# A hybrid attention and gated-linear-attention block on one Trainium2 core: another way to spread c, another order of first loads, products of zeros on TensorE, and the last output columns in two halves

## The chip, the core and the metric

The kernel runs on one core of one Trainium2 chip (trn2). The metric is the device time of one execution in microseconds (us); of several runs the median is given, beside the lowest and the highest. The profile shows one execution on the same core. Engines are named as the profile names them: PE is TensorE (PEld its weight loads), DVE VectorE, ACT ScalarE, POOL GpSimd, SP the engine that issues nearly all DMAs.

## The reference, cut to what matters

```python
mod = silu(c) @ w_cond + b_cond                 # c: (1, 2048), w_cond: (2048, 6144)
shift, scale, gate = split(mod, 3)
h = rms_norm(x) * (1 + scale) + shift           # x: (1, 512, 2048)
proj = h @ w_in                                 # 7200 columns
a_out = dilated_attention(aq, ak, av) * silu(ag)        # 16 heads of 64
g_out = rms_norm(gla_fwd + gla_bwd) * gain * silu(gg)   # 4 heads, dk 128, dv 256
y = concat(a_out, g_out) @ w_out                # (512, 2048) @ (2048, 2048)
out = rms_norm(x + gate * y) * final_gain
```

All is float32. There are 512 tokens and 2048 model columns.

## The kernel before, in words

Each float32 product is done as three products of rounded parts: a helper `three` (lines 169 to 171) adds high times high, low times high and high times low. The high part is an ACT copy into the rounded type, the low part a DVE subtraction.

**The start.** c is loaded as one row (line 181) and bcond, the bias of the conditioning, right after it (line 190). c must stand on all 128 partitions: for each quarter of 512 columns ACT rounds the row (L236), DVE takes the rest (L237), and two products with a row of ones (L238, L239) spread high and low part; ACT puts their sum through SiLU into `sb` (L240). `bcond[:, 16:32]` gets 1 added on DVE (L191). The columns of w_cond for scale come as 128x2048 tiles `cb`, one for each of 16 k-tiles; DVE multiplies a tile by `sb` and sums along the row (`cond_sum`, L244), which gives one column of scale. For k=0 this is done in four quarters. Two small products `pb` (L253) turn the relative bias into a row, which DVE combines with a constant (`bias_row_out`, L257) and ACT stores to DRAM (`grow`, L259).

**Stage a** multiplies x, scaled by (1+scale) but not yet normalised, with the 1024 value columns of w_in: for each k-tile ACT makes the high part of u (`u_high`, L347), DVE the low part (`u_low`, L350), ACT and DVE the parts of the weight tile (`w_high`, L388; `w_low`, L397; for k=0 in two halves), and PE does 8 groups j of three products (`sta`), all 8 sums staying in PSUM. DVE adds up squares of x on the way (`add_square`, L358). **Stage b** does the same for 8 further groups (`stb`) with the fully normalised h (`h_high` L378, `h_low` L381), after the sums of stage a were copied out (`v_out`, L412) and the inverse norms were made (`rstd`, L370 and L371).

The order in which ACT, DVE, SP and POOL run these steps is written out by a planner, `_plan`: each step is a task with an engine, an assumed duration, the tasks it needs, a priority, and buffers that it takes or gives back; the planner runs a clock over them, from given times at which each engine is ready, and records an order. Each engine then runs in that order, so a step that waits holds up all behind it on its engine. Weight tiles have 3 buffers for their parts and 4 for the raw load; `b8` is a pool of 8 large tiles.

**The middle** (attention, gated linear attention, gates) follows in units of 512 columns (`unit`), which the change leaves as they are.

**The end.** The output product runs in four units of 512 columns, o0 to o3. o3 runs for tokens 0 to 255, then for 128 tokens, then for the last 128. Behind each group of 128 tokens stands `finish`: DVE multiplies by the gate (L1009) and adds x (L1010), ACT squares and sums (L1012), takes Ln and Exp (L1033, L1034) for the inverse norm r, then four parts of 512 columns are multiplied by r: part 3 on DVE (L1036), parts 0 and 1 on ACT (L1037, L1039), part 2 on POOL (L1038); SP stores the four parts (L1041). In the built order POOL's part is stored first.

Of the kernel before, what the change touches and what calls it, by code (L numbers as in the profile page):

```python
# [133 lines left out]
def block_kernel(ctx: ExitStack, tc: tile.TileContext, a: dict):  # L134
# [50 lines left out]
    onesr = cst.tile([P, P], F32R, tag="ones", name="ones")  # L185
    act(onesr, one, AF.Copy)
    ones = onesr.bitcast(F32)
# [3 lines left out]
    nc.vector.tensor_scalar(bcond[:, 16:32], bcond[:, 16:32], 1.0, None, op0=ALU.add)  # L191
# [30 lines left out]
    cond_load(0, 0)  # L222
    rel = const("rel", [32, NH])
# [7 lines left out]
    c_parts = [T2(f"c_{e}", F32R) for e in range(8)]  # L231
    for j in range(4):
        ch, cl = c_parts[2 * j][64:65, :], c_parts[2 * j + 1][64:65, :]
        src = first[64:65, 512 * j:512 * j + 512]
# [5 lines left out]
        act(sb[:, 512 * j:512 * j + 512], pc, AF.Silu)  # L240

# [13 lines left out]
    def bias_row_out(j):  # L255
        t = first[:NH, 1024 + 512 * j:1536 + 512 * j]
        tt(t, pbs[j][:NH], t, op=ALU.add)  # L257
        if j:
            nc.scalar.dma_start(grow, first[:NH, 1024:2048])  # L259
# [74 lines left out]
    def sums(k, e):  # L334
# [3 lines left out]
        if k == e == 0:  # L338
            to = [part[:, z:z + 1] for z in range(3)] + [dst]
            for z in range(4):  # L340
                c = slice(512 * z, 512 * z + 512)
# [42 lines left out]
    def w_high(st, k):  # L384
        hi = wp.tile([P, 1024], F32R, tag="whi", name=f"s{st}{k}h")
        lo = wp.tile([P, 1024], F32R, tag="wlo", name=f"s{st}{k}l")
        for c in halves(st, k):
            act(hi[:, c], start_w[st, k][:, c], AF.Copy)  # L388
        spl[st, k] = hi, lo

    def halves(st, k):
        return (slice(0, 512), slice(512, 1024)) if (st, k) == ("a", 0) else (slice(0, 1024),)

    def w_low(st, k):
        hi, lo = spl[st, k]
        for c in halves(st, k):
            tt(lo[:, c], start_w[st, k][:, c], hi[:, c].bitcast(F32), op=ALU.subtract)  # L397
# [46 lines left out]
    for i, (st, k) in enumerate(sets[1:], 1):  # L444
# [4 lines left out]
        task(("w", st, k), "DMA", 1.55, [("w",) + sets[i - 1]], 1000.5 - 200 * e - 10 * k,  # L449
             lambda st=st, k=k: start_load(st, k), "raw")  # L450
    for k in range(KT):
        task(("sum", k, 0), "DVE", 2.42 if k else 3.4, [("load", k, 0)], 600 - 2 * k,
# [7 lines left out]
    for i, (st, k) in enumerate(sets):  # L460
        task(("wh", st, k), "ACT", 1.0, [("w", st, k)], 640 - i, lambda st=st, k=k: w_high(st, k), "wts")
# [3 lines left out]
    def mm_task(i):  # L465
        st, k, j = chain[i]
        need = [("ul" if st == "a" else "lo", k), ("wl", st, k)]
# [10 lines left out]
    for z in range(2):  # L478
        task(("row", z), "DVE", 0.66, [("ul", 0)], 950, lambda z=z: bias_row_out(z), None, "b8" if z else None)
# [32 lines left out]
    for i in range(2):  # L512
# [3 lines left out]
                 {"PE": 10.5, "ACT": 9.5, "DVE": 6.0, "POOL": 7.0, "DMA": 8.5})  # L516
# [326 lines left out]
    def unit(name, natural, side=(), rhs=None, lr=None, tiles=range(4)):  # L843
# [3 lines left out]
        ps = [PJ(f"ps_{name}_{i}") for i in tiles]  # L847
        pos, tick, ticks = 0, 0, 16 * len(tiles)
        for q in range(KT // 2):
# [12 lines left out]
            for n, i in enumerate(tiles):  # L862
                for kk in range(2):
                    k = 2 * g + kk
                    rh, rl = (h_hi[:, k, :], h_lo[:, k, :]) if rhs is None else rhs[k]
                    if natural:
                        t = slice(i * P, i * P + P)
                        cw = slice(kk * 512, kk * 512 + 512)
                        three(ps[n], rh[:, t], rl[:, t], hi[:, cw], lo[:, cw], q + kk == 0, q + kk == KT // 2)
# [120 lines left out]
    ssq = cst.tile([P, 4, 4], F32, tag="ssq", name="ssq")  # L990
# [14 lines left out]
    def add_up(i, ps, j):  # L1005

        x_ = x2[i][:, j, :]
        t = T2(f"y{i}{j}")
        tt(t, ps, sb[:, 512 * j:512 * j + 512], op=ALU.mult)  # L1009
        tt(x_, t, x_, op=ALU.add)  # L1010
        sq = T2(f"ysq{i}{j}")
        act(sq, x_, AF.Square, accum_out=ssq[:, i, j:j + 1])  # L1012
        if j < 3:
            nc.gpsimd.tensor_tensor(x_, x_, fgain[j], op=ALU.mult)  # L1014

    for j in range(3):
# [4 lines left out]
        for i in range(4):  # L1021
            add_up(i, ps[i], j)
# [6 lines left out]
    def finish(i, ps):  # L1029

        add_up(i, ps, 3)
# [3 lines left out]
        x_ = x2[i]  # L1035
        stt(x_[:, 3, :], x_[:, 3, :], r, fgain[3], op0=ALU.mult, op1=ALU.mult)  # L1036
        act(x_[:, 0, :], x_[:, 0, :], AF.Copy, scale=r)  # L1037
        nc.gpsimd.tensor_scalar(x_[:, 2, :], x_[:, 2, :], r, 1.0, op0=ALU.mult, op1=ALU.mult)  # L1038
        act(x_[:, 1, :], x_[:, 1, :], AF.Copy, scale=r)  # L1039
        for z in (3, 0, 2, 1):  # L1040
            nc.sync.dma_start(a["out"][i * P:i * P + P, 512 * z:512 * z + 512], x_[:, z, :])  # L1041
# [18 lines left out]
def _constants():  # L1060
# [6 lines left out]
    for window, dil in ((128, 1), (512, 4), (2048, 16)):  # L1067
# [3 lines left out]
    j, i = np.arange(P)[:, None], np.arange(P)[None, :]  # L1071
    rst = np.ones((P, 512), f)
    rst[:, ::P] = 0.0
    return {
        "ident": np.eye(P, dtype=f), "oneh": oneh, "lnm": np.tile(row, (NH, 1)),
# [4 lines left out]
def _layout(x, c, w_cond, b_cond, w_in, gla_gate_up_fwd, gla_gate_bias_fwd, gla_gate_up_bwd,  # L1080
# [6 lines left out]
    r["c"] = np.asarray(c)  # L1087
# [43 lines left out]
```

## Time and profile before

| | us |
|---|---|
| median of 3 runs | 975.26 (973.75 to 977.06) |
| the profiled execution, own time | 973.38 |
| its span in the trace | 971.6 |
| TensorE (PE) busy | 943.0 (97% of the span) |
| DVE busy | 616.6 |
| ACT busy | 441.0 |
| granted clock, mean | 0.997 |

A timeline row gives the start in us from the span's start, the duration in us, the engine, the line of the kernel, the operation, output and inputs, shapes and count (a row with x2 or more covers several that follow each other), and in brackets how long the engine had been idle and what released it. The start of an instruction on DVE or ACT can lie about 0.1 us ahead of the end of the one before it, since they overlap a little; where steps follow each other the text counts from start to start. Matmul durations overlap too, so their pitch is also counted from start to start.

### The profile page before, as it was taken

Reading aid. Unit: us, or ns where it says so; the run is one execution under the profiler, and the core shown is the slowest. Engines: PE = TensorE matmul, PEld = TensorE weight load, DVE = VectorE, ACT = ScalarE, POOL = GpSimd, SP = SyncE. Lnnn points to the kernel's source line nnn. Section 1 sums busy time; section 2 is a strip of 40 time slices with the busy share of each in tenths; the row PEclk is TensorE's granted clock in tenths of the full one; section 3 lists DMA queues with packets and bytes.
Section 4 is the critical chain, followed back from the end, with each engine's and each line's share of the span. In section 5 each row is a group of like instructions: output and inputs, shape, how many; then the busy total and the mean of one; then the engine's idle time right before and its main releaser. Section 6 shows DMA issues by size and latency. Waiting matters only on the chain.

```text
span 971.6 us, 11885 instructions
## 1 busy us (share of the span) xinstructions
PE 943.0 (97%) x4464; PEld 775.7 (80%) x4464; DVE 616.6 (63%) x916; ACT 441.0 (45%) x735; POOL 81.6 (8%) x100
## 2 busy tenths in 40 slices
PE   8999999989999999999999999999999999999996
PEld 4888788878778777778777888888888888888884
DVE  7988999566665676775534647585885352546431
ACT  5443533655655645655413544363744151333222
POOL 0000000011111122012000000000010000202120
PEclk9999999999999999999999999999999999999998
DMA  9998687422222253332444334355465455244013
GB/s 333 414 411 347 238 302 258 133 85 96 92 84 82 85 193 105 126 128 84 146 152 166 121 109 152 130 176 171 139 228 176 152 175 193 87 148 156 22 50 124
DMA packets 42619, 159.56 MB, mean 164 GB/s; under 512 B 5217, under 2 KB 5505, under 8 KB 37825
## 3 DMA queue, kind: packets, MB, share of 16 engines
q1 hardware_dynamic: 42386, 158.48, 47.2%
q8 instruction: 35, 0.57, 0.2%
q10 hardware_dynamic: 176, 0.33, 0.1%
q14 instruction: 22, 0.18, 0.1%
HBM read 154.51 MB, written 4.28 MB: 163 GB/s over the span
## 4 chain that ended last, share of the span: by engine, by line
PE 81%; DVE 8%; DMA 3%; ACT 3%; issue 3%; POOL 1%; SPq 0%; ACTq 0%; DVEq 0%; POOLq 0%
PE ps_o L170 6%; PE ps_o L171 6%; PE ps_o L169 6%; PE sta L169 3%; PE sta L170 3%; PE sta L171 3%; PE stb L171 3%; PE stb L169 3%; PE stb L170 3%; PE ps_qk L169 3%; PE ps_gv L170 3%; PE ps_gv L171 3%; PE ps_gv L169 3%; PE ps_qk L171 3%; PE ps_qk L170 3%
## 5 line engine op out<-in xcount | busy, mean ns | idle before, releaser
L585 POOL TENSOR_SCALAR p<-p,st 128x512 f32<-128x512 f32 x64 | 46.1, 721 | 424.3 <-DVE st L584 407.8
L583 ACT ACTIVATE p<-p,st 128x512 f32<-128x512 f32 x64 | 46.2, 722 | 63.4 <-DVE st L580 63.4
L244 DVE CUSTOM_DVE_ANT_0 cb<-cb,sb,c_bcond 128x2048 f32<-128x2048 f32 (+1 forms) x32 | 73.4, 2294 | 0.0
L602 DVE TENSOR_TENSOR pt<-t,pt 128x512 fp32r<-128x512 f32 x64 | 44.1, 689 | 17.8 <-ACT pt L601 17.8
L597 PE MATMUL t<-c_ident,p 128*128 128x128 f32 x256 | 38.9, 275 | 10.6 <-POOL p L585 10.6
L597 PEld LDWEIGHTS t<-c_ident,p 128*128 128x128 f32 x256 | 30.9, 140 | 22.3 <-POOL p L585 15.4
L580 DVE CUSTOM_DVE_ANT_0 p<-s,g 128x512 f32<-128x512 f32 x64 | 43.6, 686 | 7.0 <-PE s L577 6.1
L601 ACT ACTIVATE pt<-t 128x512 fp32r<-128x512 f32 x64 | 37.8, 591 | 21.1 <-PE t L597 20.5
L244 DVE CUSTOM_DVE_ANT_0 rawg<-rawg,sb,gate 128x1024 f32<-128x1024 f32 x16 | 20.7, 1294 | 27.8 <-DMA rawg<-in_wg 27.8
L611 PEld LDWEIGHTS o<-pt,vv 128*128 128x128 f32 x256 | 34.2, 189 | 3.8 <-DVE pt L602 1.7
L244 DVE CUSTOM_DVE_ANT_0 rawg<-rawg,sb,c_bcond 128x1024 f32<-128x1024 f32 x16 | 20.5, 1283 | 25.2 <-DMA rawg<-in_wg 25.2
L611 PE MATMUL o<-pt,vv 128*128 128x256 f32 x256 | 35.9, 283 | 0.0
L1014 POOL TENSOR_TENSOR x<-x,fgain 128x512 f32<-128x512 f32 x12 | 20.0, 1675 | 183.8 <-ACT ysq L1012 183.8
L1012 ACT ACTIVATE ysq<-x 128x512 f32<-128x512 f32 x16 | 10.1, 632 | 47.1 <-DVE x L1010 44.8
L767 POOL TENSOR_SCALAR dc<-st,sc 128x256 f32<-128x256 f32 x16 | 10.5, 656 | 242.5 <-DVE st L764 237.6
L584 DVE RECIPROCAL st<-st 128x1 f32<-128x1 f32 x64 | 10.4, 162 | 31.3 <-ACT p L583 31.2
L1009 DVE TENSOR_TENSOR y<-ps_o,sb 128x512 f32<-128x512 f32 x16 | 10.9, 684 | 25.9 <-PE ps_o L171 25.9
L576 PE MATMUL s<-ks,qs 128*128 128x512 f32 x64 | 25.3, 395 | 0.2 <-DVE qs L540 0.2
L577 PE MATMUL s<-kl,qs 128*128 128x512 f32 x64 | 25.0, 391 | 0.0
L774 ACT ACTIVATE sq<-st,sc 128x256 f32<-128x256 f32 x24 | 12.2, 509 | 26.2 <-DVE st L769 13.8
L618 DVE TENSOR_TENSOR cat<-o,oh 64x256 f32<-64x256 f32 x32 | 13.3, 415 | 11.9 <-ACT oh L614 11.7
L614 ACT ACTIVATE oh<-o 64x256 f32<-64x256 f32 x32 | 12.2, 380 | 17.3 <-PE o L611 16.5
(1279 smaller groups left out, 2944.6 us busy)
## 6 DMA issues: line engine op xcount, KB each, us to landing
cb<-in_wm SPq DMA_DIRECT2D x31, 1024.0 KB, 7.5
rawg<-in_wg SPq DMA_DIRECT2D x32, 512.0 KB, 3.4
raw_o<-in_w_o SPq DMA_DIRECT2D x32, 512.0 KB, 3.4
raw_qk<-in_w_qk SPq DMA_DIRECT2D x24, 512.0 KB, 3.3
rawb<-in_w_sb SPq DMA_DIRECT2D x16, 512.0 KB, 4.3
rawv<-in_wv SPq DMA_DIRECT2D x16, 512.0 KB, 3.4
raw_gv<-in_w_gv SPq DMA_DIRECT2D x16, 512.0 KB, 3.4
raw_ag<-in_w_ag SPq DMA_DIRECT2D x16, 512.0 KB, 3.4
```

The source lines that it names most:

```text
L169: mm(ps, lh, rh, start=first, stop=False)
L170: mm(ps, ll, rh, start=False, stop=False)
L171: mm(ps, lh, rl, start=False, stop=last)
L244: nc.vector.tensor_tensor_reduce(out=w, in0=w, in1=with_, op0=ALU.mult, op1=ALU.add, scale=1.0, scalar=init, accum_out=dst)
L576: mm(ps, qs[:, q], ks, start=True, stop=False)
L580: nc.vector.tensor_tensor_reduce(out=t, in0=ps, in1=gt[h][:, P * i:P * i + 512], op0=ALU.add, op1=ALU.min, scale=1.0, scalar=3e38, accum_o ...
L583: act(t, t, AF.Exp, bias=st[:, 0:1], scale=-1.0, accum_out=st[:, 1:2])
L585: nc.gpsimd.tensor_scalar(t, t, st[:, 2:3], 1.0, op0=ALU.mult, op1=ALU.mult)
L597: nc.tensor.transpose(pk[:, kt * P:kt * P + P], t[:, kt * P:kt * P + P], ident)
L601: act(hi, src, AF.Copy)
L602: tt(lo, src, hi.bitcast(F32), op=ALU.subtract)
L611: mm(po[:, :256], vv[h // 4][:, kt, h % 4, :], t[:, w, kt, :], start=kt == 0 and w == 0, stop=kt == 3 and w == 1)
```

## The change

At the start:

- c is loaded as 4 rows of 512. A constant `sel` (64 rows, 512 columns, 128 KB) is loaded before it. `crow` has 64 rows, zeros but for the four high parts (rows 0 to 3) and the four low parts (rows 32 to 35); one ACT and one DVE instruction make them. One product of `sel` and `crow` for each quarter replaces the two.
- `idle` is a tile of zeros. PE multiplies zeros by zeros (128x128 by 128x256, float32): three such products before c is ready and four behind the products of c.
- bcond is loaded after the four quarters of the first cb tile instead of before them. The addition to it, and the copy of ones, stand later in the program.
- The first sum runs in three pieces (512, 512, 1024) instead of four.
- The halves of the first weight tile are tasks of their own: the second half is rounded after `u_high(0)`. The weight load of a k-tile now has a lower priority than the cb load of the same k-tile. The store of the bias row is a task of its own on ACT, after `u_high(1)`. The times at which the planner takes the engines to be ready are earlier.

At the end: `finish` puts the multiplications of parts 0 and 2 on DVE and that of part 1 on ACT, none on POOL. The last 128 tokens of o3 run as two units of 256 columns; the first half is added up, squared and multiplied by the final gain while the second half's products run, so that behind the last product only 256 columns go through `add_up`, and there are five stores.

The built order of the changed kernel differs from the old one in two more ways, both the planner's doing. In stage a the weight parts of a k-tile are made for that k-tile and not for the one after it. And at the end of stage a, ACT runs: copies out of groups 0, `sb0h`, groups 1 and 2, rstd, group 3, rcol, groups 4, 5, 6, `sb1h`, group 7, then `h_high(0)`. Before, both `sb0h` and `sb1h` stood ahead of group 0, and `h_high(0)` ahead of group 7.

```diff
-    nc.sync.dma_start(first[64:65, :], a["c"])
-    bcond = const("bcond", [P, 48])
+    sel0 = T2("sel0", parts=64)
+    nc.sync.dma_start(sel0, a["sel"])
+    cin = T2("cin", parts=4)
+    nc.sync.dma_start(cin, a["c"])
+    idle = T2("idle")
+    nc.vector.memset(idle, 0.0)
+    crow = T2("crow", F32R, parts=64)
+    nc.vector.tensor_copy(crow, idle[:64])
+    sel = T2("sel", F32R, parts=64)
+    nc.vector.tensor_copy(sel, sel0)
...
+    def keep_on(n):
+        for _ in range(n):
+            mm(hot[:, :256], idle[:, :P], idle[:, :256], start=True, stop=True)
+    hot = PJ("hot")
+    keep_on(3)
...
     cond_load(0, 0)
+    bcond = const("bcond", [P, 48])
...
+    act(crow[0:4], cin, AF.Copy)
+    tt(crow[32:36], cin, crow[0:4].bitcast(F32), op=ALU.subtract)
     for j in range(4):
-        act(ch, src, AF.Copy)
-        tt(cl, src, ch.bitcast(F32), op=ALU.subtract)
-        mm(pc, onesr[64:65, :], ch, start=True, stop=False)
-        mm(pc, onesr[64:65, :], cl, start=False, stop=True)
+        mm(pc, sel[:, P * j:P * j + P], crow, start=True, stop=True)
         act(sb[:, 512 * j:512 * j + 512], pc, AF.Silu)
+    keep_on(4)
...
-        task(("w", st, k), "DMA", 1.55, [("w",) + sets[i - 1]], 1000.5 - 200 * e - 10 * k,
+        task(("w", st, k), "DMA", 1.55, [("w",) + sets[i - 1]], 999.5 - 200 * e - 10 * k,
...
+    for z in range(2):
+        c = slice(512 * z, 512 * z + 512)
+        task(("wh0", z), "ACT", 0.66, [("uh", 0)] if z else [], 910, lambda c=c: w_high("a", 0, c),
+             None if z else "wts")
+        task(("wl0", z), "DVE", 0.69, [("wh0", z), ("sum", 0, 0)] + ([("ul", 0)] if z else []), 899,
+             lambda c=c: w_low("a", 0, c), None, "raw" if z else None)
...
+    task("grow", "ACT", 0.4, [("row", 1), ("uh", 1)], 950,
+         lambda: nc.scalar.dma_start(grow, first[:NH, 1024:2048]), None, "b8")
...
-                 {"PE": 10.5, "ACT": 9.5, "DVE": 6.0, "POOL": 7.0, "DMA": 8.5})
+                 {"PE": 9.5, "ACT": 8.0, "DVE": 5.3, "POOL": 7.0, "DMA": 7.2})
...
-        stt(x_[:, 3, :], x_[:, 3, :], r, fgain[3], op0=ALU.mult, op1=ALU.mult)
-        act(x_[:, 0, :], x_[:, 0, :], AF.Copy, scale=r)
-        nc.gpsimd.tensor_scalar(x_[:, 2, :], x_[:, 2, :], r, 1.0, op0=ALU.mult, op1=ALU.mult)
         act(x_[:, 1, :], x_[:, 1, :], AF.Copy, scale=r)
-        for z in (3, 0, 2, 1):
-            nc.sync.dma_start(a["out"][i * P:i * P + P, 512 * z:512 * z + 512], x_[:, z, :])
+        stt(last, last, r, fgain[3][:, c], op0=ALU.mult, op1=ALU.mult)
+        nc.vector.tensor_scalar(x_[:, 0, :], x_[:, 0, :], r, None, op0=ALU.mult)
+        nc.vector.tensor_scalar(x_[:, 2, :], x_[:, 2, :], r, None, op0=ALU.mult)
+        store(3, c)
+        store(0, full)
+        store(1, full)
+        store(2, full)
+        if c.start:
+            act(x_[:, 3, c0], x_[:, 3, c0], AF.Copy, scale=r)
+            store(3, c0)
...
-    for tiles in ((0, 1), (2,), (3,)):
+    for tiles in ((0, 1), (2,)):
         ps = unit("o3", True, rhs=rhs, tiles=tiles)
         for i, p_ in zip(tiles, ps):
-            finish(i, p_)
+            finish(i, p_, slice(0, 512))
+    c = slice(0, 256)
+    ps = unit("o3", True, rhs=rhs, tiles=(3,), cut=(0, 256))
+    x_ = add_up(3, ps[0], 3, c, 4)
+    tt(x_, x_, fgain[3][:, c], op=ALU.mult)
+    stt(ssq[:, 3, 0:1], ssq[:, 3, 4:5], 1.0 / D, ssq[:, 3, 0:1], op0=ALU.mult, op1=ALU.add)
+    ps = unit("o3", True, rhs=rhs, tiles=(3,), cut=(256, 512))
+    finish(3, ps[0], slice(256, 512))
```

More of the change, by code (lines that the diff above doesn't have):

```diff
@@ L841, in block_kernel, with unit @@
     spill = []
-    def unit(name, natural, side=(), rhs=None, lr=None, tiles=range(4)):
+    def unit(name, natural, side=(), rhs=None, lr=None, tiles=range(4), cut=(0, 512)):
         side = sorted(spill + list(side), key=lambda x: x[0])
@@ L1071, in _constants @@
     j, i = np.arange(P)[:, None], np.arange(P)[None, :]
+    sel = np.zeros((64, 4, P), f)
+    for e in range(4):
+        sel[[e, 32 + e], e] = 1.0
     rst = np.ones((P, 512), f)
@@ L1074, in _constants @@
     return {
-        "ident": np.eye(P, dtype=f), "oneh": oneh, "lnm": np.tile(row, (NH, 1)),
+        "ident": np.eye(P, dtype=f), "sel": sel.reshape(64, 512), "oneh": oneh, "lnm": np.tile(row, (NH, 1)),
         "maskf": (j <= i).astype(np.int32), "rst": rst,
```

85 lines of the change are left out of this document (42 added, 43 removed).

## The prediction, made before the changed kernel ran

> **What bounds the kernel now.** First the page: its span, the busy time of PE, and the chain of work that ended last, by engine.
>
> ```profile
> span 971.6 us, 11885 instructions
> ...
> PE 943.0 (97%) x4464; PEld 775.7 (80%) x4464; DVE 616.6 (63%) x916; ACT 441.0 (45%) x735; POOL 81.6 (8%) x100
> ...
> PE 81%; DVE 8%; DMA 3%; ACT 3%; issue 3%; POOL 1%; SPq 0%; ACTq 0%; DVEq 0%; POOLq 0%
> ```
>
> PE works 97% of the span, so only its gaps, slow products and the two ends can be won. The change touches three such places: the start up to the second k-tile of stage a, the passage from stage a to stage b (through the planner), and the tail. The timeline of the start:
>
> ```profile
> 3.43 0.43 SPq L176 DMA_DIRECT2D c_rel<-in_rel  x1
> ...
> 5.76 0.75 DVE L244 CUSTOM_DVE_ANT_0 cb<-cb,sb,c_bcond 128x512 f32<-128x512 f32 x1
> ...
> 6.65 0.75 DVE L244 CUSTOM_DVE_ANT_0 cb<-cb,sb,part 128x512 f32<-128x512 f32 x1
> ...
> 8.14 3.57 PE L253 MATMUL pb<-first,c_rel 32*16 32x512 f32 x4 [0.81 <-DMA first<-in_oneh]
> ...
> 9.11 0.08 DVE L244 DVE_READ_ACCUMULATOR2_ANT scale<- 128x1 f32 x1
> ...
> 10.42 1.29 ACT L388 ACTIVATE sa0h<-rawa 128x512 fp32r<-128x512 f32 x2 [2.46 <-DMA rawa<-in_w_sa]
> ...
> 11.61 0.71 ACT L347 ACTIVATE h_hi<-xt,scale 128x512 fp32r<-128x512 f32 x1
> 12.35 0.75 DVE L350 SCALAR_TENSOR_TENSOR h_lo<-xt,scale,h_hi 128x512 fp32r<-128x512 f32 x1
> ...
> 12.37 0.80 PE L169 MATMUL sta<-sa0h,h_hi 128*128 128x512 f32 x1 [0.66 <-ACT h_hi L347]
> ...
> 14.66 1.27 DVE L257 TENSOR_TENSOR first<-pb,first 16x512 f32<-16x512 f32 x2
> ...
> 15.86 2.33 DVE L244 CUSTOM_DVE_ANT_0 cb<-cb,sb,c_bcond 128x2048 f32<-128x2048 f32 x1
> ...
> 16.73 0.63 PE L169 MATMUL sta<-sa0h,h_hi 128*128 128x512 f32 x1
> ...
> 17.16 0.54 PE L170 MATMUL sta<-sa0h,h_lo 128*128 128x512 f32 x1
> ...
> 18.13 0.67 DVE L358 TENSOR_TENSOR ssum<-ssum,sq 128x512 f32<-128x512 f32 x1
> ...
> 18.73 1.21 DVE L397 TENSOR_TENSOR sa2l<-rawa,sa2h 128x1024 fp32r<-128x1024 f32 x1
> ...
> 19.86 0.73 DVE L350 SCALAR_TENSOR_TENSOR h_lo<-xt,scale,h_hi 128x512 fp32r<-128x512 f32 x1
> ...
> 20.52 0.39 PE L169 MATMUL sta<-sa1h,h_hi 128*128 128x512 f32 x1
> ...
> 20.75 0.40 PE L170 MATMUL sta<-sa1h,h_lo 128*128 128x512 f32 x1
> ```
>
> Scale of k=0 was ready at 9.19, but the weight tile landed only at 10.42, and both halves were rounded before `h_hi`; so products began at 12.37. They ran at a pitch of 0.43 us (16.73 to 17.16) until about 17.2, then at 0.23 (20.52 to 20.75). The second k-tile needed its low part, which DVE finished at 20.59: slow products and DVE's queue end at the same time there, and from then on PE runs on.
>
> **The start, step by step.** Three things set the new time.
>
> (1) *bcond.* It is now issued right behind the four cb quarters, where rel was.
>
> ```profile
> c_bcond<-in_bcond SPq DMA_DIRECT2D x1, 24.0 KB, 1.6
> ...
> c_rel<-in_rel SPq DMA_DIRECT2D x1, 2.0 KB, 4.2
> ...
> lrb<-in_w_lr SPq DMA_DIRECT2D x1, 256.0 KB, 2.8
> ```
> ```profile
> 5.00:6.00 1.00, 1.00 (x4) 0.80 (x3) 0.97 (x3) 0.74 (x2) 0.00 (x0) 1.00 1.09 412
> ```
>
> Ahead of the cb tile it landed in 1.6 us; rel, behind it, in 4.2: 3.43 + 4.2 = 7.6. sel's 128 KB at 412 GB/s (the last figure of the window 5 to 6) add 0.3: 7.9. This is bounded by 5.0 (1.6 us after issue) and about 8.7 (sel twice as dear and small packets). sel, half of lrb's size, lands within lrb's 2.8 us of an issue at about 0.7, so by 3.5; its copy, two small steps, ACT's rounding and DVE's subtraction (some 2.2 us) bring the products of c to about 5.6 and the last quarter of `sb` to about 9, where the third sum needs it at 9.9: a delay of up to 0.9 us is hidden by bcond. The sums: the addition 0.2, then two pieces at 0.89 (5.76 to 6.65) and one of 1024 columns. A piece of 512 takes 0.75, one of 2048 takes 2.33, so 512 more cost 0.53, and 1024 take 1.28 + 0.08. Scale is ready at 7.9 + 0.2 + 1.78 + 1.36 = 11.2, two us later than before.
>
> (2) *The first weight half*, 10.42 + 0.3 = 10.7. Its rounding (0.65) ends at 11.35, then `h_hi` until 12.07: PE begins at 12.1 instead of 12.37. So an early bcond would gain hardly anything, and a late one costs one for one.
>
> (3) *DVE.* From 12.1: `h_lo` 0.67 to the next start, the second weight half 0.63, two rows 1.2 (14.66 to 15.86), the sum of k=1 2.27 (15.86 to 18.13), `sa1l` 1.14 (18.73 to 19.86, the row of `sa2l`), `h_lo` 0.73: 18.75. Gone from this stretch are the squares (18.13 to 18.73) and `sa2l`, which now come later. The second product of k=1 is released at 18.8 instead of 20.75: **1.95 us earlier**, if PE is done with k=0 by then. After its `h_lo` at 12.85 PE has 22 products left: at 0.23 us they end at 17.9 and the step holds; at 0.43 they end at 22.3. So the zeros decide. Afterwards DVE needs 2.27 + 0.60 + 1.14 + 0.67 = 4.68 us for a k-tile and PE 24 x 0.227 = 5.44, so PE stays fed; loads ran at 412 GB/s, 4.5 us for the 1.84 MB of a k-tile.
>
> *The zeros.* pb, four rows of two float32 products of 512 columns, takes 3.57 us, so a product of 256 takes 0.9 slow, 0.45 fast. Three run from about 1.5 (behind two memsets) to 4.1; c's four from about 5.5 to 7.2; four zeros until 10.8 if all is slow. pb follows: 14.4 if slow, by about 11.5 if fast. The trace shows that pb (32 rows by 16 columns) and c's one-row products did not bring the fast pitch: PE was busy with them from 3.3 to 11.7, and `sta` was still slow. It came 4.8 us after `sta` began, with all 128 rows in use. The zeros use all rows; 4.8 us after 5.5 is 10.3, before `sta`. I take the fast pitch. The granted clock in the windows reads 1.00 in both states, so only the pitch shows it. [...] No run here shows whether zeros count.
>
> **From stage a to stage b.**
>
> ```profile
> 96.74 1.06 ACT L388 ACTIVATE sb1h<-rawb 128x1024 fp32r<-128x1024 f32 x1 [3.77 <-issue]
> 97.70 2.54 ACT L412 ACTIVATE vraw<-sta 128x512 f32<-128x512 f32 x4
> ...
> 103.97 0.71 ACT L378 ACTIVATE h_hi<-xt,shift 128x512 fp32r<-128x512 f32 x1
> 104.58 0.59 ACT L412 ACTIVATE vraw<-sta 128x512 f32<-128x512 f32 x1
> ...
> 105.06 0.72 ACT L378 ACTIVATE h_hi<-xt,shift 128x512 fp32r<-128x512 f32 x1
> ...
> 104.73 0.50 PE L169 MATMUL stb<-h_hi,sb0h 128*128 128x512 f32 x1 [0.61 <-ACT h_hi L378]
> ```
>
> Here PE waits for `h_hi(0)`, and ACT is the chain. `h_hi(0)` started one step behind the copy of group 6. In the new order `sb1h` (0.96, 96.74 to 97.70) and the copy of group 7 (0.48, 104.58 to 105.06) stand between them. Group 6 can't be copied before PE has ended it, and `sb0h` (another 0.96) among the earlier copies fits, as pss comes a group earlier. So stage b starts **1.45 us later** relative to the end of stage a. The bounds are 1.2 (overlap) and 2.4 (`sb0h` doesn't fit either). DVE's `h_lo(0)` follows as before. Stage b has no gap in which this could be made up.
>
> **The tail.**
>
> ```profile
> 453.74 1.10 PE L611 MATMUL o<-pt,vv 128*128 128x256 f32 x8
> 454.67 0.40 PE L169 MATMUL ps_gk<-h_hi,gk5h 128*128 128x512 f32 x1
> ...
> L611 PEld LDWEIGHTS o<-pt,vv 128*128 128x128 f32 x256 | 34.2, 189 | 3.8 <-DVE pt L602 1.7
> ...
> L769 DVE SCALAR_TENSOR_TENSOR st<-kv,sc,dc 128x256 f32<-128x256 f32 x16 | 7.7, 483 | 7.9 <-POOL dc L767 6.9 <-PE ps_gv L170 0.6 <-ACT gg06h L313 0.3
> ...
> 962.27 0.69 DVE L1009 TENSOR_TENSOR y<-ps_o,sb 128x512 f32<-128x512 f32 x1 [7.29 <-PE ps_o L171]
> ...
> 964.81 0.20 ACT L1034 ACTIVATE rn<-rn 128x1 f32<-128x1 f32 x1
> 965.04 0.72 ACT L1037 ACTIVATE x<-x,rn 128x512 f32<-128x512 f32 x1
> ...
> 965.17 1.18 POOL L1038 TENSOR_SCALAR x<-x,rn 128x512 f32<-128x512 f32 x1 [9.63 <-ACT rn L1034]
> ...
> 966.38 1.79 SPq L1041 DMA_DIRECT2D out<-x  x4
> ```
>
> PE: 96 products of 256 columns instead of 48 of 512, each with a weight load. L611 is that form: eight from 453.74 to 454.67, 0.117 each, so 11.2 to 11.3 against 48 x 0.227 = 10.9: **+0.4**. If loads didn't overlap (0.189 each) it would be 18.1, +7.2. Behind PE: a DVE step of 256 takes 0.48 against 0.75 (h_lo's form), so two save 0.54, and the square about 0.2: **-0.75** of the 2.75 from 962.27 to r at 965.02. The stores: the first waited for POOL until 966.35, 1.36 after r. Now it waits for one DVE step of 256, 0.52 after r; but the next waits for another DVE step. 1 MB at 412 GB/s is 2.5 us, so the stores are limited by their data as much as by issue (0.45 each): between 0.15 (the last issue) and 0.85 (the first) is gained; I take **-0.6**, nearer to the first, as the last store is half as large. The tail gives -0.95 in all, -1.2 to -0.5 by these bounds.
> [...]
>
> **Sum.** -1.95 + 1.45 - 0.95 = -1.4 us on the profiled execution's own 973.38 (span 971.6 and 1.8 around it), 972.0. That execution lies 1.9 below the median of the runs, 975.26; the forecast for a median is 975.26 - 1.4 = **973.9**.
>
> **Rivals.**
> [...]
> - *The weight loads of the halves don't overlap*: +6.8 more, 980.7. Against it: L611's pitch.
> - *The passage costs nothing*, because something else holds PE there anyway: -1.95 - 0.95 = -2.9; if also the weight half lands at 10.4 as before, -3.2: 972.1. Against it: ACT runs in order, and PE's last gap there ended on `h_hi`.
> - *bcond or sel late* by 1.5 us: the start gains 0.45, in all 0.1: 975.4, no change.
>
> **How the numbers follow.** Forecast 0.66 (its own range 972.3 to 975.5), slow zeros 0.13, weight loads 0.03, the better case 0.12, late loads 0.06. 0.3% is 2.9 us, about what a measurement can tell from no change. Faster by more: two thirds of the better case and the edge of the forecast, 0.13. Slower: the weight loads and two thirds of the slow zeros, 0.12. Within: 0.75. The range runs from the better case, less the 1.5 by which the lowest run lay under the median, to the slow zeros: 970.6 to 977.8.
>
> **What would show it.** Right: `sta` starts at 12 with a pitch of 0.23; the second product of k=1 at 18.8; `h_hi(0)` of stage b behind `sb1h` and group 7, a gap of about 2.2 us before `stb`; 0.117 a product in the last unit; the first of the last stores 0.5 after r. Wrong: a pitch of 0.43 after 12.1, pb ending past 13, scale later than 11.7, or a pitch above 0.13 at the end.

## The result, and the profile after

The changed kernel takes 976.46 us (median of 20 runs, 973.88 to 981.54) against 974.2 us of the kernel before (20 runs, 972.26 to 977.06): ratio 1.0032, 95% interval 1.0019 to 1.0046. It is slower by 0.3%, where 1.4 us less were forecast (973.9 from the 975.26 of the first three of these runs of before). The profiled execution took 978.51 us and lies high among its runs, 5.1 us above the profiled one of before; the medians differ by 2.3. Its page:

```profile
span 976.7 us, 12006 instructions
...
PE 949.3 (97%) x4522; PEld 782.3 (80%) x4522; DVE 619.8 (63%) x926; ACT 436.1 (45%) x731; POOL 77.4 (8%) x96
```

PE's busy time grew by 6.3 us, and the zeros alone are 6.7 (2.93 and 3.78 below); its share stays at 97%, so the page doesn't show where the time went. The timeline of the start:

```profile
1.49 2.93 PE L200 MATMUL hot<-idle 128*128 128x256 f32 x6 [1.49 <-DVE idle L187]
...
7.49 3.78 PE L200 MATMUL hot<-idle 128*128 128x256 f32 x8
...
8.01 0.18 DVE L252 TENSOR_SCALAR c_bcond<-c_bcond 128x16 f32<-128x16 f32 x1 [2.57 <-DMA c_bcond<-in_bcond]
...
11.20 3.59 PE L268 MATMUL pb<-first,c_rel 32*16 32x512 f32 x4
...
11.43 0.72 ACT L361 ACTIVATE h_hi<-xt,scale 128x512 fp32r<-128x512 f32 x1
...
14.72 0.80 PE L169 MATMUL sta<-sa0hi,h_hi 128*128 128x512 f32 x1
...
18.73 0.63 PE L169 MATMUL sta<-sa0hi,h_hi 128*128 128x512 f32 x1
...
22.47 0.39 PE L169 MATMUL sta<-sa1hi,h_hi 128*128 128x512 f32 x1
```

bcond and `h_hi` came as forecast (`h_hi` is done at 12.15), but pb ran slowly and held PE until 14.7. The first k-tile was slow again until about 19.4, and the second began at 22.47 (before: 20.52): +1.95 where -1.95 was forecast.

The passage to stage b, by the timeline, and then a window with PE's granted clock (the column ahead of the DMA share):

```profile
105.88 1.05 ACT L401 ACTIVATE sb1hi<-rawb 128x1024 fp32r<-128x1024 f32 x1
106.83 0.59 ACT L420 ACTIVATE vraw<-sta 128x512 f32<-128x512 f32 x1
...
107.31 1.33 ACT L392 ACTIVATE h_hi<-xt,shift 128x512 fp32r<-128x512 f32 x2
...
108.08 0.78 PE L169 MATMUL stb<-h_hi,sb0hi 128*128 128x512 f32 x1 [2.05 <-ACT h_hi L392]
...
111.84 0.39 PE L169 MATMUL stb<-h_hi,sb0hi 128*128 128x512 f32 x1
```
```profile
108.00:111.50 3.50, 3.42 (x8) 2.62 (x9) 3.50 (x4) 1.58 (x3) 0.00 (x0) 0.52 0.68 239
```

`sb1hi` and the copy of group 7 stand ahead of `h_hi(0)` as forecast, and the wait grew from 0.61 to 2.05. Stage b is 3.4 us late when it begins, of which the passage is 1.4. Then something not forecast: behind the gap the clock stood at a half until 111.5 (0.52 in the window, 1.00 in those beside it), and the first k-tile of stage b took 7.2 us (108.1 to 115.3) instead of 5.9 (104.7 to 110.6), +1.3. The running difference is 4.7 us there, between 4.1 and 5.0 until 590 us, 5.3 behind a wait of 0.95 us for DVE's `at` at 679 us, and 6.0 before the tail; at the end it is 5.1. The tail gave back 0.9:

```profile
968.44 0.28 PE L170 MATMUL ps_o<-o36h,c_l 128*128 128x256 f32 x1
968.56 0.28 PE L171 MATMUL ps_o<-o36l,c_h 128*128 128x256 f32 x1
968.87 0.42 DVE L1028 TENSOR_TENSOR y<-ps_o,sb 128x256 f32<-128x256 f32 x1 [3.80 <-PE ps_o L171]
...
970.66 0.20 ACT L1055 ACTIVATE rn<-rn 128x1 f32<-128x1 f32 x1
970.89 0.48 DVE L1061 SCALAR_TENSOR_TENSOR x<-x,rn,fgain 128x256 f32<-128x256 f32 x1 [1.14 <-ACT rn L1055]
...
971.30 0.48 DVE L1063 TENSOR_SCALAR x<-x,rn 128x512 f32<-128x512 f32 x1
971.41 2.30 SPq L1058 DMA_DIRECT2D out<-x  x5
```

The pitch is 0.12 a product, so the last unit ends 0.6 us later than it would in one piece. Then r is ready 2.0 us after the first step behind PE (before: 2.75), and the first store goes out 0.55 after r instead of 1.36.

### The profile page after: what moved, and what is told of

It reads as the page before. It is cut to its first block, busy times and chain, and to the rows that moved or that the text cites. A ratio compares the mean times of both kernels' runs of the same rounds, so it can differ in the third digit from the quotient of the medians.

```text
span 976.7 us, 12006 instructions
## 1 busy us (share of the span) xinstructions
PE 949.3 (97%) x4522; PEld 782.3 (80%) x4522; DVE 619.8 (63%) x926; ACT 436.1 (45%) x731; POOL 77.4 (8%) x96
## 4 chain that ended last, share of the span: by engine, by line
PE 76%; DVE 10%; DMA 5%; ACT 4%; issue 4%; POOL 1%; DVEq 0%; POOLq 0%; ACTq 0%
PE ps_o L170 6%; PE ps_o L169 6%; PE ps_o L171 6%; DMA rawg<-in_wg 4%; PE ps_qk L169 3%; PE sta L169 3%; PE stb L169 3%; PE ps_qk L171 3%; PE ps_qk L170 3%; PE stb L170 3%; PE sta L170 3%; PE stb L171 3%; PE sta L171 3%; PE ps_gv L171 3%; PE ps_gv L170 3%
## 5 line engine op out<-in xcount | busy, mean ns | idle before, releaser
L1032 ACT ACTIVATE ysq<-x 128x512 f32<-128x512 f32 (+1 forms) x17 | 10.3, 606 | 48.8 <-DVE x L1029 46.8
L1028 DVE TENSOR_TENSOR y<-ps_o,sb 128x512 f32<-128x512 f32 (+1 forms) x17 | 11.1, 653 | 23.6 <-PE ps_o L171 23.6
```

## The experiments

**Parts of the change (e1 to e4).** e1 is the changed kernel without zeros, e2 the changed kernel with the passage as it was, e3 the kernel before with the new tail, e4 has both edits of e1 and e2.

```diff
# e1: the changed kernel, and e4 too
-    hot = PJ("hot")
-    keep_on(3)
...
-    keep_on(4)
# e2: the changed kernel, and e4 too; ahead of the call of _plan
+    for name in (("wh", "b", 1), ("vo", 7)):
+        tasks[name][2].append(("hi", 0))
```

> The changed kernel without the seven products of zeros. Theory: in the changed kernel they ran slow (four from 7.5 to 11.3) and pushed pb to 11.2 and the first sta to 14.7. Without them pb starts at about 8.5, when its load lands, and ends by 12.1; sta starts at about 12.3 with the slow pitch, and the second k-tile at about 20.3 instead of 22.5. All else stays: the gap ahead of stb and the slow products behind it (+2.7 against before) and the shorter tail (-0.9). Against before about +1.5 us (ratio 1.0015), against the changed kernel about -2. Rival, that the later bcond and the new order of loads are what delays the start: sta still begins past 14, ratio as the changed kernel's, 1.003.

> The changed kernel with two more dependencies in the planner: sb1h and the copy of group 7 come after the first high part of stage b on ACT. Theory: the gap ahead of stb falls from 2.2 to about 0.8 us and the slow products behind it go too (the first k-tile of stb takes 5.9 instead of 7.2): -2.7 us against the changed kernel, ratio to before about 1.0005. Rival, that the slow products of stb have another cause than the gap: the gap goes but the first k-tile still takes 7.2, -1.4. Rival, that stage b has slack: no change in time.

> The kernel before with the change of the tail alone (last 128 tokens in two halves, the scaling by r on DVE and ACT, five stores). Theory: -0.9 us, ratio 0.999: 96 products at 0.12 cost 0.6, the 256-column steps save 0.75 and the stores 0.75. Rival, that the halves cost more in weight loads or that DVE's extra steps stand in the way: ratio 1.001 or more.

> Both: no zeros, and the passage as in e2. Theory: the start about as before (second k-tile at about 20.3), the passage as before, the tail -0.9: -1 us against before, ratio 0.999. Rival, loads: the start at 22.5, ratio 1.001 or more.

Measured against before: e1 976.76 us, ratio 1.0019 (1.0004 to 1.0035); e2 974.3 us, 1.0001 (0.9988 to 1.0014); e3 973.22 us, 0.9991 (0.9982 to 1.0001); e4 973.71 us, 1.0002 (0.9984 to 1.002). The tail is worth about what was forecast (-0.95 of 974 is a ratio of 0.9990). The passage is what makes the change slower: without it 0.3% go, and stage b waits 0.61 us again and not 2.05 (103.15 below). In the profile of e1 the first product begins at 12.41 and the second k-tile at 19.73, so the rival of that run, a start held up by its loads, falls. The zeros make no difference that can be measured, with or without the passage. That is not because they do nothing. The timeline of e2, whose program is the changed kernel's up to this point:

```profile
7.47 3.31 PE L200 MATMUL hot<-idle 128*128 128x256 f32 x8
...
10.71 1.89 PE L268 MATMUL pb<-first,c_rel 32*16 32x512 f32 x4
...
18.55 0.39 PE L169 MATMUL sta<-sa1hi,h_hi 128*128 128x512 f32 x1
...
103.15 0.50 PE L169 MATMUL stb<-h_hi,sb0hi 128*128 128x512 f32 x1 [0.61 <-ACT h_hi L392]
```

Here the zeros turned fast on their way, pb took 1.89 us, and the second k-tile came at 18.55, as the prediction wanted. The same instructions do one thing in one execution and another in the next. And e1, which has the same gap of 2.05 us ahead of stage b, ran on fast behind it, but not behind a later gap where PE waits for POOL's `p`; that gap is in the kernel before too (3.04 us, ending at 207.00):

```profile
105.35 0.50 PE L169 MATMUL stb<-h_hi,sb0hi 128*128 128x512 f32 x1 [2.05 <-ACT h_hi L389]
...
207.61 1.12 PE L612 MATMUL t<-c_ident,p 128*128 128x128 f32 x4 [2.96 <-POOL p L600]
208.38 0.78 PE L169 MATMUL ps_qk<-h_hi,qk21h 128*128 128x512 f32 x1
```

So slow products come and go behind gaps, by something that the program doesn't seem to set; the runs on the clock alone show what it is.

**The clock by itself (e5, e6).** Both kernels hold nothing but products on PE and DVE steps that make it wait: `gap(ps, k)` puts k steps of 512 columns and two more between two products. Behind each gap e5 has a single product that ends the wait, then 22, 22, 10, 10, 5 and 22 products of the form, and 10 of float32r with 128 rows. Each of the two was run once.

```python
for form in ("zeros_r", "halves_r", "zeros_f32", "halves_f32", "rows32_f32", "rows64_r"):   # e5, 7 times
    gap(ps, 26 + rep % 3)
    ...
for k in (3, 6, 1, 5, 2, 7, 4, 0):   # e6, 5 times, behind 8 copies of the changed start
    gap(ps, k)
    ps = real(28)
```

> Leaves out the whole computation: only PE's warm-up forms, 7 times each in turn, each after some 10 us without products, with 10 real products (float32r, 128 rows, 512 columns) behind each. What is asked: from when on do the products run at the fast pitch (0.23 us for 512 columns of float32r instead of 0.43; 0.45 us for a float32 product of 256 columns instead of 0.94)? In six profiles so far the first k-tile turned fast 3.2 to 5.3 us after its first product in five kernels, with and without zeros before it; in one (the changed kernel with the passage mended) it came during the second zeros, some 10.3 us after the start, with the same program up to there as in the changed kernel, where it came at 19.4. Theory P (any product of 128 rows counts, and the moment lies differently from execution to execution): zeros and halves, float32r and float32, all turn fast between 3 and 7 us after their start in all 7 copies, and the spread over the copies is some 3 us in each form. Theory Z (zeros as data don't count): zeros_r and zeros_f32 stay at 0.43 and 0.94 through their 9.4 us, the halves turn. Theory F (float32 products don't count): zeros_f32 and halves_f32 stay slow, zeros_r turns. By all of them 32 rows by 16 columns stay slow (products of 1.79 us), as pb's 3.6 us did in five of six profiles; 64 rows are open.

> Leaves out the whole computation. First, 8 copies of the changed start's products, each after some 10 us without products: three zeros, a gap of about 1 us, four products of 64 rows, four zeros, two of 32 rows, then 26 real products. Then 40 bursts of 28 real products with gaps between them that grow from about 1 to about 4 us, 5 of each size, in mixed order. Theory P (the moment is a matter of luck): in 2 to 6 of the 8 copies the real products begin at 0.23 us, in the others they turn 3 to 5.5 us after their start, as in the profiles. Theories Z and F (zeros or float32 don't count): none of 8 begins fast. The gaps: in the profiles a gap of 2.9 to 3.06 us was followed by 2 to 6 us of slow products in three of six cases, one of 1.84 to 2.05 us in two of five, none of 0.5 to 1.5 us. Theory P: none of the gaps under 1.5 us, some of those of 2 us, half or more of those of 3 us and all of 4 us are followed by a slow stretch. Rival G (the slow stretches came from something else, not from the gap): they don't grow with the gap's length.

e5, the windows of the first copy of each form in the order above, and the ten float32r products behind the last:

```profile
25.00:31.58 6.58, 6.58 (x23) 5.30 (x22) 0.00 (x0) 0.00 (x0) 0.75 0.00 0
47.71:54.84 7.13, 7.13 (x23) 5.68 (x22) 0.00 (x0) 0.00 (x0) 0.68 0.00 0
70.97:77.65 6.68, 6.68 (x21) 5.42 (x20) 0.00 (x0) 0.00 (x0) 0.61 0.01 2
93.98:99.41 5.43, 5.43 (x21) 4.55 (x20) 0.00 (x0) 0.00 (x0) 0.76 0.00 0
115.90:124.54 8.64, 8.64 (x11) 1.29 (x11) 0.00 (x0) 0.00 (x0) 0.50 0.00 0
142.21:151.89 9.68, 9.68 (x24) 7.06 (x23) 0.00 (x0) 0.00 (x0) 0.50 0.00 0
151.89:155.73 3.84, 3.84 (x11) 2.73 (x10) 0.00 (x0) 0.00 (x0) 0.64 0.00 0
```

The first four forms all turn fast on their way (mean clock 0.61 to 0.76), in every copy. Zeros (0.75 in float32r, 0.61 in float32) did it, and so did halves (0.68 and 0.76): theories Z and F fall. Thirty-two rows stay at 0.50 for 8.6 us, as expected. Sixty-four rows, which were open, stay at 0.50 for 9.7 us: products of the form of c's new ones did not open the clock by themselves.

In e6 all eight copies of the start turned fast before the real products; 2 to 6 had been expected. Their starts lay within 1 us of each other against the points described below, so they were not eight independent cases. The gaps, four of the forty bursts of 28 products (start, length; in brackets the gap):

```profile
326.51 8.27 PE L172 MATMUL real<-halfr,w 128*128 128x512 f32 x28 [2.89 <-DVE w L166]
335.82 6.64 PE L172 MATMUL real<-halfr,w 128*128 128x512 f32 x28 [1.04 <-DVE w L166]
344.89 6.64 PE L172 MATMUL real<-halfr,w 128*128 128x512 f32 x28 [2.43 <-DVE w L166]
355.35 9.28 PE L172 MATMUL real<-halfr,w 128*128 128x512 f32 x28 [3.81 <-DVE w L166]
```

A burst without slow products takes 6.64. None of the ten gaps of 1.04 and 1.51 us was followed by slow products, four of five of 1.97, none of five of 2.43, all five of 2.89, two of five of 3.35, and all ten of 3.81 and more. So a gap of 2 us can do it (rival G falls), and its length doesn't decide alone.

**Gaps filled (e7).** The kernel before with 23 idle products, where PE waits for `p`:

```diff
                 pk = PA(f"t{h}{i}")
+                for _ in range(FILL.get(tiles_seen[0], 0)):      # FILL = {0: 12, 38: 4, 48: 3, 54: 4}
+                    mm(pk, h_hi[:, 0, :P], h_hi[:, 1, :], start=True, stop=True)
+                tiles_seen[0] += 1
```

> The kernel before with 23 idle products (first rows of h_hi, into the PSUM tile that the transposes then overwrite) ahead of four of the transposes of p where PE waited for POOL: 12 (2.7 us) where the wait was 2.9 to 3.1 in every profile, 4, 3 and 4 where it was 0.8 to 2.0. The output is that of the kernel before. Theory P (a gap can be followed by slow products, by luck): nothing is lost, as PE waits there anyway, and the slow stretches behind these gaps, which cost 1.2 to 2.7 us in three of the six profiles, don't come any more: the median falls by 0.5 to 1.5 us (ratio 0.9985 to 0.9995), and the runs lie closer together. Rival G: within 0.3 us of the kernel before, or slower by up to 1 us where the idle products delay the transposes.

972.84 us (971.44 to 974.96) beside 974.03 of before: ratio 0.9983 (0.9964 to 1.0002). The size is the expected one, though the interval still touches 1.

```profile
204.09 2.99 PE L599 MATMUL t<-h_hi 128*128 128x512 f32 x12 [0.50 <-DVE kl L553]
206.91 0.60 PE L602 MATMUL t<-c_ident,p 128*128 128x128 f32 x4
```

The gap is gone, and the transposes begin at 206.91, no later than before's 207.00.

**Versions that leave no gap, and the changed kernel again (e8 to e12).** e8 has the passage of e2, the filled gaps of e7, and zeros without a hole (sel, too, gets 128 rows; rows 64 to 127 of both are zero); e9 is the changed kernel once more; e10 is e4 with the gaps filled; e11 is e3 with the gaps filled; e12 is the changed kernel with only the zeros altered.

```diff
# e8 and e12, beside the changed kernel
-    keep_on(3)
+    keep_on(4)
...
-    crow = T2("crow", F32R, parts=64)
+    crow = T2("crow", F32R)
...
-    keep_on(4)
+    keep_on(6)
```

> The changed kernel with four edits. The copies of stage a wait for the passage as in the second experiment. The zeros are made to leave no hole: four instead of three ahead of c's products, c's products with 128 rows instead of 64 (rows 64 to 127 of both operands zero), six instead of four zeros behind them. The 23 idle products ahead of the transposes, as in the filled kernel. The output is that of the changed kernel. Theory W (the clock is set at points 3.41 us apart, which don't start with the kernel, and opens where the 3.41 us before such a point held more than some 2.0 to 2.4 us of products of 128 rows; it closes where they held more than about 1.5 to 2.0 us without): from 1.5 us on PE has 9 us of products of 128 rows, so the clock is open before 8.5 us wherever the points lie, pb takes 1.9 us and not 3.6, the first product of stage a begins at 12.0 to 12.6 at a pitch of 0.23, and the second k-tile at 18.5 to 18.9. Gains against before: 1.5 to 2.0 at the start, 1.0 at the tail, 1.0 to 1.5 by the filled gaps: 970 us, ratio 0.995 to 0.997. Rival L (luck has no share, the added instructions of the start cost what they gain): ratio 0.998 to 1.000, as the filled kernel alone.

> The changed kernel itself once more, for a second look at the same program. Theory W: the start has room for about three in four placings of the points in which the second zeros (7.5 to 11.2) open the clock; so pb takes 1.9 us rather than 3.6, the first product of stage a begins at 12.5 and the second k-tile at 18.5 to 19.0 with a chance of 0.74, as in the profile of the second experiment; else 14.7 and 22.5 as in the first profile. Behind the gap of 2.05 us before stage b a slow stretch with a chance of about a half. Rival (the changed kernel's start is slow by its program): 14.7 and 22.5 again, and stage b slow again.

> The changed kernel without any zeros at the start, the passage mended, and the 23 idle products. Theory W: stage a begins at 12.2 to 12.4 with slow products for 2.3 to 5.8 us (the first point behind at least 2.3 us of its own products), the second k-tile at 19.6 to 20.8; gains against before 0.3 at the start, 1.0 at the tail, 1.0 to 1.5 by the filled gaps: 971.5 us, ratio 0.997 to 0.998, and 1.0 to 1.5 us behind the version with zeros without a hole. Rival L: no different from that version.

> The kernel before with the changed tail and the 23 idle products; the old start and passage. Theory W: 1.0 by the tail and 1.0 to 1.5 by the filled gaps: 972 us, ratio 0.997 to 0.998. The version with zeros without a hole is 1.5 to 2.0 us faster than this one if the start is worth what the prediction gave it. Rival L: the two agree.

> The changed kernel with zeros that leave no hole (four, c's products with 128 rows, six) and nothing else: the passage waits for 2.05 us as in the changed kernel, and the later gaps aren't filled. The changed kernel's twenty times fall into 973.9 to 976.5 (eleven) and 977.8 to 981.5 (nine); both of its profiles were of the upper part, with the start at 14.7 and the second k-tile at 22.5. Theory W (the upper part is above all the start that didn't open the clock, 3.9 us at the second k-tile against 18.6 with an open clock): the first product begins at 12.0 to 12.6 and the second k-tile at 18.2 to 18.9, the upper part shrinks to single runs, and the median falls by 1 to 2 us to 974.5 to 975.5 (ratio 1.000 to 1.002). Rival V (the upper part comes from slow stretches behind the passage and the later gaps, which stay): the two parts stay, and the median is 976 to 976.5 (ratio 1.002 to 1.003).

e8: 972.2 us (970.74 to 973.04), ratio 0.9973 (0.9959 to 0.9986). It is faster than both kernels, and its twelve runs lie within 2.3 us, where the changed kernel's twenty spread over 7.7. The start did what was wanted (pb took 1.88 us):

```profile
12.09 0.49 PE L170 MATMUL sta<-sa0hi,h_hi 128*128 128x512 f32 x1
...
18.22 0.39 PE L170 MATMUL sta<-sa1hi,h_hi 128*128 128x512 f32 x1
```

But the gain is 1.8 us by the medians (2.6 by the ratio) where 4 had been expected. e10 gave 972.99 (0.9983, 0.9968 to 0.9997) and e11 973.4 (0.9986, 0.9971 to 1.0001), where 971.5 and 972 had been expected. So all three fell short, by 1.4 to 2.2 us. In the profile of e10 bcond came late (its addition began at 8.99), and the second k-tile at 21.90 and not at 19.6 to 20.8. e8 lies 1.2 us ahead of e11, where its start was to be worth 1.5 to 2.0. The order of the three is as expected, and their intervals overlap, so the worth of the start is not settled by them.

e9, the changed kernel again, at 978.36 us:

```profile
11.29 3.59 PE L268 MATMUL pb<-first,c_rel 32*16 32x512 f32 x4
...
22.45 0.39 PE L169 MATMUL sta<-sa1hi,h_hi 128*128 128x512 f32 x1
```

pb was slow again, the second k-tile came at 22.45, and stage b, at 108.06, was slow again behind its gap of 2.05. By itself this speaks for the rival of that run, a start that is always slow. Against it stands e2, whose start is the same and was fast; e13 asks how often.

e12: 975.92 us (970.71 to 978.24), ratio 1.0011 (0.9997 to 1.0026). The median lies between the ranges of its two theories, the ratio inside that of theory W, and its interval over both, so it doesn't tell them apart. Two of twelve runs lie above 977.8 (nine of twenty in the changed kernel). Its profile shows why the start is still not safe:

```profile
10.22 1.89 PE L269 MATMUL pb<-first,c_rel 32*16 32x512 f32 x4
13.38 0.50 PE L169 MATMUL sta<-sa0hi,h_hi 128*128 128x512 f32 x1 [1.27 <-ACT h_hi L362]
```
```profile
10.95:14.36 3.41, 1.85 (x5) 0.47 (x4) 3.09 (x7) 2.38 (x4) 0.00 (x0) 1.00 0.97 390
14.36:17.77 3.41, 3.41 (x9) 2.64 (x9) 3.41 (x4) 1.59 (x3) 0.00 (x0) 0.50 1.04 426
```

The zeros had opened the clock, but bcond landed 1.2 us later than in the first profile, and pb (1.16 us of it in the first window) together with the wait of 1.27 let the clock shut for one stretch of 3.41 us in the middle of the first k-tile.

**How often (e13).** One execution, with twenty copies of the changed start at spread places, then twenty gaps of 1.97 us and twenty of 2.89 between bursts of different lengths.

```python
for rep in range(20):
    gap(ps, 24 + rep % 8)
    ...
for rep in range(20):
    for k in (2, 4):
        gap(ps, k)
        ps = real(28 + (5 * rep + 3 * k) % 16)
```

> Leaves out the whole computation. 20 copies of the changed start's products (three zeros, a gap of 0.8 to 1.1 us, four products of 64 rows, four zeros, two of 32 rows, 26 real products), each after 12 to 16 us without products, in eight lengths, so that they meet the clock's points (3.41 us apart) at many places; in the earlier eight copies the starts lay within 1 us of each other against the points, and all eight opened. Then 20 gaps of about 2.0 us and 20 of about 2.9 us, in turn, between bursts of 28 to 43 real products. Theory W with the bounds from the profiles so far (opens if the 3.41 us before a point hold more than 2.0 to 2.4 us of products of 128 rows; closes if they hold more than 1.5 to 2.0 us without): the copies open before the real products in 60 to 90% (12 to 18 of 20), and those that don't are the ones whose points lie badly; the gaps of 2.0 us are followed by a slow stretch of 3.4 us in 35 to 65%, those of 2.9 us in 70 to 95%. Rival A (the start opens always in such a copy, and something else in the changed kernel keeps the clock shut): 20 of 20. Rival B (the length of the gap alone decides): all or none of each size.

Two of the copies, one shut and one open, by the timeline:

```profile
180.50 3.78 PE L178 MATMUL z<-zero 128*128 128x256 f32 x8
184.22 3.59 PE L184 MATMUL pb<-half 32*16 32x512 f32 x4
...
243.72 2.93 PE L178 MATMUL z<-zero,w 128*128 128x256 f32 x6 [15.35 <-DVE w L166]
247.52 1.16 PE L184 MATMUL pc<-halfr,w 64*128 64x512 f32 x4 [0.87 <-DVE w L166]
```

In the first the second zeros are slow to the end, and so is pb. In the second the clock opened at 247.32, behind the first zeros and ahead of c's products, which took 1.16 instead of 2.04. Twelve of twenty copies had an open clock ahead of the real products, eight had not. Ten of twenty gaps of 1.97 us were followed by a shut clock, and sixteen of twenty of 2.89 us. Rivals A and B fall. In windows of 0.5 us the clock changed 92 times; the first of these two rows is an opening (0.50 before it, 1.00 after), the second a shutting:

```profile
32.20:32.70 0.50, 0.50 (x3) 0.23 (x1) 0.00 (x0) 0.00 (x0) 0.91 0.00 0
...
45.90:46.40 0.50, 0.00 (x0) 0.00 (x0) 0.47 (x2) 0.00 (x0) 0.54 0.00 0
```

From the share of such a window follows the moment: 0.91 means that 0.41 of the 0.50 us were fast, so the clock opened at 32.29; by the last row it shut at 45.94. That is 13.65 us, or 4.00 steps of 3.413. All 92 moments of this trace, from 15.22 to 1117.72, lie on whole steps of 3.4133 us to within 0.03, a length fitted to them. Set against these points the copies and the gaps fall into place. Counted by the rows, whose ends are modelled, the clock opened where one step held at least 2.69 us of products of 128 rows, and not at 2.61 or less (theory W had 2.0 to 2.4). It shut in every step with 1.97 us or more without such products and in none with 1.90 or less; at 1.95 and 1.96 it did both. The edges are good to about 0.1 us: in e1 a gap of 1.84 shut it too, at 421.91.

The same points account for the kernels' own profiles. By the share in the row below, the clock shut at 108.13 in the changed kernel:

```profile
108.00:108.40 0.40, 0.32 (x1) 0.32 (x2) 0.40 (x2) 0.40 (x2) 0.00 (x0) 0.66 0.90 369
```

Counted back in steps of 3.4133, the points at the start lie at 2.31, 5.73, 9.14, 12.55, 15.97 and 19.38. The zeros fill 2.1 us of the step that ends at 5.73, 1.65 of the next and 2.1 of the one to 12.55, never 2.6; so the clock opened only at 19.38, behind a step full of stage a's products. In e2 the clock shut at 204.74, which puts points at 3.36, 6.77 and 10.18: the zeros from 7.47 on fill 2.71 us of the step that ends at 10.18, and pb came out fast. The wait of 2.05 us ahead of stage b lies in one step in the changed kernel (104.71 to 108.13) and shut the clock. In e1 a point at 104.47 divides the same wait into 1.17 and 0.88, and the clock stayed open.

## Why the prediction was wrong, point by point

The step that failed is "So the zeros decide. [...] I take the fast pitch": it is right that the zeros decide, but they decide by where they fall. The prediction counted 4.8 us from c's products on, as if the clock had a delay behind the first product. e13 showed points 3.41 us apart, and they don't start with the kernel (counted back, one lies at 2.31 in the changed kernel's profile, at 3.36 in e2's). It showed too that c's products of 64 rows did not do for products of 128: in the shut copy above they and the zeros filled the step that ends at 182.48 (1.44 and 1.97 us), and the clock stayed shut. Whether they count in part is not shown. What is left are 2.9 us of zeros from 1.5 and 3.7 from 7.5, of which 2.6 to 2.7 must fall into one step (by e13's 2.61 and 2.69); that happened in 12 of 20 placings in e13, and in one of the three profiles of a kernel with this start. So the start has a chance, where the forecast gave it a time.

- *The slow zeros* had a chance of 0.13 and the top of the range, 977.8. No run shows the 0.13; in e13 the clock was still shut ahead of the real products in 8 of 20 placings. No run shows 977.8, 2.5 above 975.26, as their price either; the measured start, passage and tail (+1.95, +1.44 and -0.9) add up to 2.5 too, without the 1.3 behind the passage, and the two profiled executions with this start shut took 978.51 and 978.36 us. Zeros do count (e5); these fell badly. pb, worked out to end at 14.4 if slow, held PE until 14.7, and the second k-tile came at 22.47 and 22.45 (e9).
- *With an open clock the start is as forecast*: the second product of the second k-tile at 19.06 (e2) and 18.73 (e8) against 18.8. The steps on bcond (8.01), scale (11.4) and the weight half (10.66) hold in the first profile. Yet bcond's addition began between 7.89 and 9.19 in the eight profiles with the new start, so "late loads" is a case of its own in each execution, of 0.5 us in the mean.
- *The passage* costs 1.44 us (2.05 less 0.61), as forecast. What the prediction lacked is a term: a gap of 2 us can shut the clock (ten of twenty gaps of 1.97 us in e13), and then 1.3 us more are lost (7.2 us for the first k-tile, not 5.9). "Stage b has no gap in which this could be made up" was right; that the new gap would make its products slower was not seen. So the passage is the second term that failed: +1.45 in the sum, some 2.1 by these figures.
- *The tail* gives 0.9 (0.95 forecast; e3 0.9991). Two terms missed and cancel, by luck: PE's halves cost 0.6, not 0.4, and the stores give 0.75, not 0.6 (parts 0 and 2 took 0.48 us each on DVE, where a step of that size in `h_lo`'s form takes 0.75). The step to r gives 0.75 as worked out.
- *The sum.* With the measured shares: start 0.6 x (-1.95 + 0.5) + 0.4 x 1.95 = -0.1; passage 1.44 + 0.5 x 1.3 = 2.1; tail -0.9. That is +1.1 us. It is a mean over lucky and unlucky starts, and the means of the runs differ by 3.2 (ratio 1.0032; the medians by 2.3, and the interval begins at 1.9). So about 2 us stay open, or 1 at the edge of the interval. Half of them are in e2 and e4 too: -1.0 is worked out for the tail and the start without the passage, and 1.0001 and 1.0002 were measured, with intervals that reach 0.9988 and 0.9984. The profiles show where such differences arise: PE's waits for `p` at 416 to 422 us were 0.8 us in some executions and 1.9 in others, the gap that ends at 205 to 212 us was followed by slow products in e1, e2, e4 and e12 and not in before, e3 or the two of the changed kernel, and a wait of 0.95 to 1.6 us for `at` at 675 to 681 us stands in some of them. Whether the change makes these more frequent, or whether they fell so, was not settled.

The range held the median of the runs, which is partly luck: it reaches up to 977.8 only for the slow zeros, and nine of the twenty runs lie above that. The sign was wrong, and the chance of slower (0.12) too small.

## What to carry to other kernels

Ask of each wait on TensorE not only how long it is but whether it can shut the clock: here a gap of 2.05 us cost 1.44 us beside one of 0.61, and 1.3 more where the clock shut behind it (half of the gaps of 1.97 us in e13), and filling a gap of 3.04 us with idle products cost nothing: the transposes behind it began at 206.91 (e7), where they had begun at 207.00. Products meant to open the clock should use all 128 rows (those of 64 left it at 0.50 for 9.7 us in e5) and run without a hole for some 5.4 us (an estimate: twice the 2.69 us of e13, so that one of its steps of 3.41 us holds enough wherever the points lie). Shorter or broken, they are a lottery ticket (12 of 20 in e13), and when they don't work they stand in the way (pb at 11.20 for 3.59 us in the changed kernel, at 10.71 for 1.89 in e2). If a kernel's times spread more after a change than before (7.7 us against 4.8), look for such a lottery before explaining one profile: here the same start gave opposite findings in the profiles of the changed kernel and of e2.

## What the runs showed of the hardware

- In e13 the granted clock changed 92 times, each within 0.03 us of a whole number of steps of 3.4133 us. There it opened with 2.69 us of products of 128 rows in a step, not with 2.61, and shut with some 1.9 to 2.0 us without them; a gap of 1.97 us was enough in ten of twenty cases, one of 2.89 in sixteen of twenty.
- Products of 64 rows and 128 columns in float32r left the clock at 0.50 for 9.7 us, and those of 32 rows by 16 columns for 8.6 (e5); with an open clock, pb and a wait of 1.27 us were followed by 3.41 us at 0.50 (e12). Zeros opened it, and so did halves (mean clock 0.75 and 0.68 in float32r, 0.61 and 0.76 in float32, e5).
- At the start of the profiled executions the granted clock reads 1.00 although the products run slowly (in the changed kernel at a pitch of 0.43 us from 16.2 to 18.7, against 0.23 from 19.7 on). Behind the passage the reading agrees with the pitch (0.52 from 108 to 111.5 us in the changed kernel, where the first product of stage b took 0.78 us and that at 111.84 took 0.39).
- A float32 multiplication by a value of each row, on DVE from SBUF to SBUF, took 0.48 us for 128x512 (971.30 in the changed kernel), where `h_lo` took 0.75 and the addition to `ssum` 0.68 (means of before).
